# Pairs 14 and 15 computed first and plain in the up projection, the Strassen pairs 0 to 13 after them

## The chip, the cores and the metric

One core of a Trainium2 chip runs the kernel. The metric is the time of the device in microseconds; the median of several runs is compared. TensorE is called PE in the profile, VectorE DVE, ScalarE ACT, GpSimd POOL, and SyncE, which issues every DMA here, SP.

## What is computed

One decoder layer on 1024 tokens of 1024 features in float32. The part that matters is its second half, the MLP, and the norms about it:

```
h = rmsnorm(x, norm_ffn_g[l])
x = x + jnp.square(jax.nn.relu(h @ w_ffn_up[l])) @ w_ffn_down[l]
...
return rmsnorm(x, norm_final_g)
```

The hidden width is 4096, that is 32 tiles of 128, or 16 pairs of tiles.

## The kernel before

The first half (norm, input projection, attention, convolution, output projection) is not touched. Every product of float32 matrices is made of three matmuls of rounded parts (`mm3`, lines 58 to 61): high with high, high with low, low with high. The high part is rounded by ACT (line 55), the low part is the difference and is made by DVE or POOL (line 56, the split).

The up projection goes over 16 pairs of hidden tiles. A pair with its two halves of tokens is a 2 x 2 block product, and 14 pairs are computed by a Strassen scheme with seven products instead of eight (`up7`, line 986, products u1 to u7 of 12 matmuls of 128x512 each). The scheme needs sums of the activations as moving operands (t1s, t2s, t4s and new contents of h2h[1] and h2l[1]). They are built from a copy of the activations in DRAM (`hraw`), in `make_moving` (line 966) and `make_t3` (line 975): loads into the seven buffers `tmp`, subtractions on POOL, rounding on ACT, low parts on DVE. Until they are there, two pairs are computed plainly (`up_plain`, line 917, with `up_half`, eight products' worth of matmuls); before the change these are pairs 0 and 1. `NPL = 2` at line 1067 is their number.

What a pair yields goes to DRAM in `hid[1]` to `hid[7]`, in the form in which the down projection needs it. `sums_up` (line 895) makes it: four squared blocks a11, a21, a12, a22 in the tile `work_q`, and four sums s1 to s4 of them in `work_s` (lines 906, 907, 908, 914, on DVE), seven stores in all. For pairs 14 and 15 the sums are left out and four blocks are stored plainly (`plain`, line 899).

The down projection takes two pairs as a group: eight groups, of which the first seven use a Strassen scheme again, and the last, group 7 of pairs 14 and 15, is plain and is fused with the last norm (`final`). `SEQ0`, `SEQ`, `SEQN` give the order of the seven products of a group. For each product, `load_b` and `load_h` fetch a weight block b and a hidden block h, `prep` (line 1057) splits both into high and low, and `products` (line 1129) makes four token tiles in two PSUM tiles of two banks each, named dn + group + product + first token tile (dn060 and dn062 are product 6 of group 0). There are four such PSUM tiles at a time (`ps_two`, line 865). Products 1, 6 and 7 of group 0 are copied to `xe` by ACT (line 1138); all others are added by DVE to an accumulator (line 1140): products 2 and 3 to the tiles xr0 and xr1, products 4 and 5 to xr2 and xr3, one for each two token tiles. These four hold x, which `reload_x2` (line 1111) fetches from DRAM again, since their memory was lent out during the up projection: xr0's to `work_q`, xr1's to `work_s` (line 881), those of xr2 and xr3 to t4s. Line 1160 subtracts the accumulators from each other once, when product 5 of group 0 is due.

`begin_down` (line 1082) is called in the last pair after its third product, and loads and splits the first blocks of group 0.

Within each engine the order of instructions is settled when the program is built, by a scheduler that follows its own estimate of time; DMAs are issued by SP in such an order too, and an instruction that waits holds up those behind it on its engine.

Of the kernel before, what the change touches and what calls it, by code (L numbers as in the profile page):

```python
# [33 lines left out]
def body(tc, x, norm_mix_g, w_in, b_forget, conv_dw_w, conv_dw_b, conv_ln_g, conv_ln_b,  # L34
# [19 lines left out]
    def split(hi, lo, src, eng=V):  # L54
        A.activation(hi, src, AF.Copy)  # L55
        eng.tensor_tensor(lo, src, f32(hi), op=ALU.subtract)  # L56

    def mm3(ps, sh, sl, mh, ml, first, last):
        T.matmul(ps, sh, mh, start=first, stop=False)  # L59
        T.matmul(ps, sh, ml, start=False, stop=False)  # L60
        T.matmul(ps, sl, mh, start=False, stop=last)  # L61
# [4 lines left out]
    def ps_mm(name):  # L66
        return psum.tile([P, HN], F32, tag="mm", name=name, bufs=4)
# [669 lines left out]
    for t in range(NT):  # L737
        n = CV0 + CVS * t
# [23 lines left out]
    with tc.manual_schedule(engines={mybir.EngineType.PE}):  # L762
        for n in range(START, len(units) + 30):
# [4 lines left out]
            if 0 <= n < len(units):  # L768
                weighted_v(n, *prs.pop(n))
                h, hf, kt = units[n]  # L770
# [17 lines left out]
    def load_w2(src, name, shape, scale=None):  # L788
        hi = wgt.tile(shape, F32R, tag="hi", name=name + "h", bufs=3)
        lo = wgt.tile(shape, F32R, tag="lo", name=name + "l", bufs=3)  # L790
        half = shape[1] // 2
        for k in range(0, shape[1], half):
            raw = wgt.tile([P, half, shape[2]], F32, tag="raw", name=f"{name}r{k}", bufs=3)
            SP.dma_start(raw, src[:, k:k + half, :])
            if scale is None:
                split(hi[:, k:k + half, :], lo[:, k:k + half, :], raw)
            else:
                for j in range(half):
                    A.activation(hi[:, k + j, :], raw[:, j, :], AF.Copy, scale=chan(scale, k + j))
                    V.scalar_tensor_tensor(lo[:, k + j, :], raw[:, j, :], chan(scale, k + j), f32(hi[:, k + j, :]),  # L800
                                           op0=ALU.mult, op1=ALU.subtract)
        return hi, lo
# [44 lines left out]
    def norm_cols2(t):  # L847
        xn = xns.pop(t)
        pt = ps_big(f"n2_{t}_t")
        for k in range(KT):  # L850
            T.transpose(pt[:, k * P:(k + 1) * P], xn[:, k * P:(k + 1) * P], ident)
        hf, c = t // 4, (t % 4) * P
        split(h2h[hf][:, :, c:c + P], h2l[hf][:, :, c:c + P], pt.rearrange("p (k n) -> p k n", k=KT))
        A.activation(x2[t], pt, AF.Copy)
        SP.dma_start(hraw[:, :, t * P:(t + 1) * P].rearrange("k p n -> p k n"), x2[t].rearrange("p (k n) -> p k n", k=KT))
# [9 lines left out]
    def ps_two(name):  # L865
        return psum.tile([P, 2, HN], F32, tag="two", name=name, bufs=4)

    NPAIR = NFF // 2
# [6 lines left out]
    def load_up(j):  # L875
        return load_w2(w_up_k[:, :, j * P:(j + 2) * P], f"up{j}", [P, KT, 2 * P])
# [3 lines left out]
    def open_work():  # L880
        work["q"] = x2p.tile([P, 2, 2, HN], F32, tag="x0", name="work_q", bufs=1)
        work["s"] = x2p.tile([P, 4, HN], F32, tag="x1", name="work_s", bufs=1)

    def up_half(p, w, e, hf, ps):
        sl = slice(e * P, (e + 1) * P)
        for k in range(KT):
            mm3(ps, w[0][:, k, sl], w[1][:, k, sl], h2h[hf][:, k, :], h2l[hf][:, k, :], k == 0, k == KT - 1)
        q = work["q"][:, e, hf, :]
        A.activation(q, ps, AF.Relu)
        A.activation(q, q, AF.Square)  # L890
# [4 lines left out]
    def sums_up(p, last):  # L895
        q, sm = work["q"], work["s"]
        a11, a21, a12, a22 = q[:, 0, 0, :], q[:, 0, 1, :], q[:, 1, 0, :], q[:, 1, 1, :]
        s1, s2, s3, s4 = [sm[:, i, :] for i in range(4)]
        plain = p >= NPAIR - 2
        if not last:  # L900
            store(p, 1, a11)
            store(p, 4, a22)
            if plain:
                store(p, 0, a21)
                return
            V.tensor_tensor(s1, a21, a22, op=ALU.add)
            V.tensor_tensor(s2, s1, a11, op=ALU.subtract)
            V.tensor_tensor(s3, a11, a21, op=ALU.subtract)
            for i, a in ((5, s1), (6, s2), (7, s3)):
                store(p, i, a)  # L910
        else:
            store(p, 2, a12)
            if not plain:
                V.tensor_tensor(s4, a12, s2, op=ALU.subtract)
                store(p, 3, s4)

    def up_plain(p, w, hfs):
        for hf in hfs:
            for e in range(2):
                up_half(p, w, e, hf, ps_two(f"up{p}{e}{hf}")[:, 0, :])  # L920
            if (p, hf) == (NPL - 1, 1):
                for k in range(4):
                    make_t3(k)
        sums_up(p, False)
        sums_up(p, True)

    def load_up7(p):
        g = [wgt.tile([P, 2, 4, P], F32, tag="raw", name=f"ur{p}{i}", bufs=3) for i in range(3)]
        ah, al, bh, bl = [wgt.tile([P, 4, 4, P], F32R, tag=tg, name=f"u{tg}{p}{c}", bufs=3) for c in "ab" for tg in ("hi", "lo")]
        c0 = 2 * p * P  # L930
        for dst, k0, e in ((g[2][:, 0], 0, 1), (g[2][:, 1], 4, 1), (g[0][:, 0], 0, 0), (g[1][:, 1], 4, 0)):
            SP.dma_start(dst, w_up_k[:, k0:k0 + 4, c0 + e * P:c0 + (e + 1) * P])
        G.tensor_tensor(g[0][:, 1], g[2][:, 0], g[2][:, 1], op=ALU.add)  # L933
        G.tensor_tensor(g[1][:, 0], g[0][:, 1], g[0][:, 0], op=ALU.subtract)
        G.tensor_tensor(g[2][:, 0], g[0][:, 0], g[2][:, 0], op=ALU.subtract)
        split(ah[:, 0:2], al[:, 0:2], g[0])
        split(ah[:, 2:4], al[:, 2:4], g[1])
        G.tensor_tensor(g[1][:, 1], g[1][:, 1], g[1][:, 0], op=ALU.subtract)  # L938
        split(bh[:, 0], bl[:, 0], g[1][:, 1])
        split(bh[:, 1:3], bl[:, 1:3], g[2])  # L940
        w = {1: (ah, al, 0), 5: (ah, al, 1), 6: (ah, al, 2), 2: (ah, al, 3), 3: (bh, bl, 0), 7: (bh, bl, 1), 4: (bh, bl, 2)}
        return {i: (h[:, j], l[:, j]) for i, (h, l, j) in w.items()}
# [15 lines left out]
    def tmp(name):  # L958
        return tp.tile([P, HN], F32, tag="tmp", name=name, bufs=7)
# [15 lines left out]
    def make_t3(k):  # L975
        b12, b22 = load_hraw(f"c12_{k}", k, 1), load_hraw(f"c22_{k}", 4 + k, 1)
        G.tensor_tensor(b12, b22, b12, op=ALU.subtract)
        split(*mov[7][k], b12)

    def prod(p, w, i):  # L980
        ps = ps_two(f"u{i}_{p}")[:, 0, :]
        for k in range(4):
            mm3(ps, w[i][0][:, k, :], w[i][1][:, k, :], *mov[i][k], k == 0, k == 3)
        return ps

    def up7(p, w, mid=None):
        q = work["q"]
        s1, s5, u2 = tmp(f"us1_{p}"), tmp(f"us5_{p}"), tmp(f"uu2_{p}")

        def relu2(dst, ps, other):  # L990
            V.tensor_tensor(dst, ps, other, op=ALU.add)  # L991
            V.scalar_tensor_tensor(dst, dst, 0.0, dst, op0=ALU.max, op1=ALU.mult)  # L992

        A.activation(s1, prod(p, w, 1), AF.Copy)
        A.activation(s5, prod(p, w, 5), AF.Copy)
        V.tensor_tensor(u2, prod(p, w, 6), s1, op=ALU.add)
        if mid is not None:
            mid()
        G.tensor_tensor(s5, s5, u2, op=ALU.add)
        relu2(q[:, 0, 0, :], prod(p, w, 2), s1)  # L1000
        relu2(q[:, 0, 1, :], prod(p, w, 3), s5)
        p7 = prod(p, w, 7)
        V.tensor_tensor(u2, p7, u2, op=ALU.add)
        relu2(q[:, 1, 1, :], p7, s5)
        sums_up(p, False)
        relu2(q[:, 1, 0, :], prod(p, w, 4), u2)
        sums_up(p, True)
# [57 lines left out]
        return hi, lo  # L1065

    NPL = 2
    uws = {0: load_up(0)}
    open_work()
    for e in range(2):  # L1070
        up_half(0, uws[0], e, 0, ps_mm(f"up0{e}0"))
    norm_cols2(NT - 1)
    pn.release()
    psum.release()
# [15 lines left out]
        load_h(0, SEQ0[3])  # L1090
        ready[0] = prep(*steps[0])

    for p in range(NPAIR):
        if p + 1 < NPAIR:
            uws[p + 1] = load_up(2 * p + 2) if p + 1 < NPL else load_up7(p + 1)
        if p < NPL:
            for k in range(2 * p, 2 * p + 2):
                make_moving(k)
            up_plain(p, uws.pop(p), (1, 0) if p else (1,))
        else:  # L1100
            up7(p, uws.pop(p), begin_down if p == NPAIR - 1 else None)
    tp.release()
    hp.release()

# [137 lines left out]
```

## Time and profile before

| | us |
|---|---|
| median of 3 runs | 1165.04 |
| lowest and highest run | 1164.96 and 1166.43 |
| the profiled execution | 1163.59 |
| its span, from the first to the last instruction | 1161.9 |
| PE busy | 1123.3 |
| DVE busy | 913.7 |
| ACT busy | 471.6 |
| POOL busy | 466.1 |

The span is one execution on the chip taken by the profiler; the execution's own time is 1.7 us longer than the span. A busy time is the sum of an engine's instructions, over stages that are limited by different things, so the stretch at hand has to be looked at. In this execution the up projection begins at about 515 us of the span, its Strassen pairs at 568, and the down projection at 838.

### The profile page before, as it was taken

The numbers are of one execution on the slowest core, as the hardware profiler recorded it, in microseconds if no ns is written. First come the engines' busy times: TensorE is split into PE (matmuls) and PEld (weight loads), VectorE is DVE, ScalarE is ACT, GpSimd is POOL, SyncE is SP. The second block draws the span as 40 slices with busy tenths as digits, with TensorE's granted clock in tenths as the row PEclk, the third lists the DMA queues.
The fourth block names the chain that finished last, engine by engine and source line by source line (L and its number), as shares of the span: only waits on it lengthen the run. The fifth ranks groups of instructions, "written<-read, shape, count | busy, mean of one in ns | idle before, by whom it ended". The sixth has DMA issues, their size and how long they took to land. (4 is left out here: it accounts for less than half of the span.)

```text
span 1161.9 us, 15112 instructions
## 1 busy us (share of the span) xinstructions
PE 1123.3 (97%) x5455; PEld 915.3 (79%) x5455; DVE 913.7 (79%) x1147; ACT 471.6 (41%) x723; POOL 466.1 (40%) x358
## 2 busy tenths in 40 slices
PE   6999999999999999999899999999999999999997
PEld 6899888866677778887688888888877888888876
DVE  5399999666888765565887878787699988888994
ACT  6322353128788932364422222222253333333422
POOL 6122254116878820124743434343263434352021
PEclk9999999999999999999999999999999999999999
DMA  8021136683423333456644444444694454445003
GB/s 260 16 74 37 37 83 155 174 234 92 128 83 87 105 129 125 141 170 209 217 143 163 137 163 142 158 146 171 223 396 149 162 175 156 142 137 173 27 23 123
DMA packets 121779, 164.52 MB, mean 142 GB/s; under 512 B 9112, under 2 KB 66792, under 8 KB 121704
## 3 DMA queue, kind: packets, MB, share of 16 engines
q1 hardware_dynamic: 121704, 163.56, 43.5%
q8 instruction: 43, 0.70, 0.2%
q14 instruction: 32, 0.26, 0.1%
HBM read 114.67 MB, written 48.79 MB: 141 GB/s over the span
## 5 line engine op out<-in xcount | busy, mean ns | idle before, releaser
L292 DVE SCALAR_TENSOR_TENSOR conv<-u,par,conv 128x1024 f32<-128x1024 f32 x108 | 133.7, 1280 | 1.7 <-ACT conv L287 1.3
L1140 DVE TENSOR_TENSOR xr<-dn,xr 128x1024 f32<-128x1024 f32 x56 | 67.8, 1217 | 22.6 <-PE dn L61 22.6
L56 POOL TENSOR_TENSOR pl<-pt,ph 128x512 fp32r<-128x512 f32 (+3 forms) x71 | 74.6, 1066 | 25.3 <-ACT ph L55 22.2
L938 POOL TENSOR_TENSOR ur<-ur 128x512 f32<-128x512 f32 x14 | 23.1, 1647 | 95.4 <-DVE ulo10a L56 7.4
L613 ACT ACTIVATE pt<-sT,ctok 128x512 f32<-128x512 f32 (+1 forms) x96 | 54.5, 585 | 11.5 <-PE sT L611 5.8
L992 DVE SCALAR_TENSOR_TENSOR work_q<-work_q 128x512 f32<-128x512 f32 x56 | 53.1, 947 | 1.0
L453 DVE CUSTOM_DVE_ANT_0 mj<-s,ck 128x512 bf16<-128x512 f32 (+2 forms) x64 | 37.4, 585 | 18.6 <-PE s L447 11.6
L991 DVE TENSOR_TENSOR work_q<-u,us 128x512 f32<-128x512 f32 x42 | 28.6, 681 | 26.7 <-PE u L61 26.7
L55 ACT ACTIVATE ph<-pt 128x512 fp32r<-128x512 f32 (+1 forms) x96 | 48.7, 530 | 0.6
L1140 DVE TENSOR_TENSOR xe<-dn,xe 128x1024 f32<-128x1024 f32 x36 | 42.8, 1213 | 3.6 <-PE dn L61 3.6
L82 POOL TENSOR_SCALAR rs_tmp<-n_ss 128x1 f32<-128x1 f32 x16 | 5.6, 347 | 87.5 <-ACT n_xn L116 80.6
L59 PE MATMUL qk<-hTh,wh_qk 128*128 128x512 f32 x96 | 39.0, 406 | 0.0
L60 PE MATMUL qk<-hTl,wh_qk 128*128 128x512 f32 x96 | 37.9, 395 | 0.0
L61 PE MATMUL qk<-hTh,wl_qk 128*128 128x512 f32 x96 | 37.8, 394 | 0.0
L445 PE MATMUL s<-ks,q 128*128 128x512 f32 (+2 forms) x96 | 36.6, 388 | 0.9 <-DVE m L453 0.8
L633 PE MATMUL av<-pl,v 128*65 128x512 f32 (+1 forms) x96 | 32.5, 339 | 3.9 <-POOL pl L56 2.3
L61 PE MATMUL v<-wh_v,hTl 128*128 128x260 f32 x128 | 36.1, 282 | 0.0
L60 PE MATMUL v<-wl_v,hTh 128*128 128x260 f32 x128 | 36.1, 282 | 0.0
L59 PE MATMUL v<-wh_v,hTh 128*128 128x260 f32 x128 | 36.0, 281 | 0.0
L631 PE MATMUL av<-ph,v 128*65 128x512 f32 (+1 forms) x96 | 35.3, 368 | 0.1
L933 POOL TENSOR_TENSOR ur<-ur 128x512 f32<-128x512 f32 x14 | 24.0, 1717 | 24.8 <-DVE up2l L56 3.0
L608 PE MATMUL sT<-q,ks 128*128 128x512 f32 (+1 forms) x96 | 33.6, 350 | 0.1
(1315 smaller groups left out, 3908.1 us busy)
## 6 DMA issues: line engine op xcount, KB each, us to landing
h<-hid SPq DMA_DIRECT2D x53, 512.0 KB
b<-in_w_ffn_down SPq DMA_DIRECT2D x32, 512.0 KB
ur<-in_w_ffn_up SPq DMA_DIRECT2D x56, 256.0 KB
hid<-work_s SPq DMA_DIRECT2D x56, 256.0 KB
hid<-work_q SPq DMA_DIRECT2D x50, 256.0 KB
xp<-in_x SPq DMA_DIRECT2D x8, 512.0 KB
qstack<-qk SPq DMA_DIRECT2D x32, 128.0 KB
kstack<-qk SPq DMA_DIRECT2D x32, 128.0 KB
```

What stands on the lines that cost most here:

```text
L55: A.activation(hi, src, AF.Copy)
L56: eng.tensor_tensor(lo, src, f32(hi), op=ALU.subtract)
L59: T.matmul(ps, sh, mh, start=first, stop=False)
L60: T.matmul(ps, sh, ml, start=False, stop=False)
L61: T.matmul(ps, sl, mh, start=False, stop=last)
L292: V.scalar_tensor_tensor(dst, u[:, k:k + S], tap_w(c, k), cell[0], op0=ALU.mult, op1=ALU.add)
L445: T.matmul(ps[:, :w], d["q2"][:, i * P:(i + 1) * P], d["ks"][:, b0:b1], start=True, stop=b1 < n)
L453: V.tensor_tensor_reduce(junk[:, :w], ps[:, :w], d["ck"][:, b0:b1], op0=ALU.subtract, op1=ALU.max, scale=1.0, scalar=d.pop("m0") if b0 els ...
L613: A.activation(pt[:, :w], ps[:, :w], AF.Exp, bias=ctok[:, h * NT + kt:h * NT + kt + 1])
L631: T.matmul(av[:DH + 1, o0:], v1, ph[:, :w], start=kt == ORDER[hf][0], stop=False)
L992: V.scalar_tensor_tensor(dst, dst, 0.0, dst, op0=ALU.max, op1=ALU.mult)
L1140: V.tensor_tensor(a, ps, a, op=ALU.add)
```

## The change

The order of the pairs becomes 14, 15, 0, 1, ..., 13, and the two pairs computed plainly are 14 and 15. Their weights are both requested before the loop (the call for the second was in the loop), and `up_plain` is told by a flag, no longer by the pair's number, when to make the last moving operands. With it, the pairs that are plain in the up projection are those that have no sums, and the last two pairs of the up projection, now 12 and 13, have them.

```diff
@@ -914,11 +914,11 @@
                 V.tensor_tensor(s4, a12, s2, op=ALU.subtract)
                 store(p, 3, s4)
 
-    def up_plain(p, w, hfs):
+    def up_plain(p, w, hfs, last):
         for hf in hfs:
             for e in range(2):
                 up_half(p, w, e, hf, ps_two(f"up{p}{e}{hf}")[:, 0, :])
-            if (p, hf) == (NPL - 1, 1):
+            if last and hf == 1:
                 for k in range(4):
                     make_t3(k)
         sums_up(p, False)
@@ -1065,10 +1065,12 @@
         return hi, lo
 
     NPL = 2
-    uws = {0: load_up(0)}
+    order = list(range(NPAIR - NPL, NPAIR)) + list(range(NPAIR - NPL))
+    pa, pb = order[:NPL]
+    uws = {pa: load_up(2 * pa), pb: load_up(2 * pb)}
     open_work()
     for e in range(2):
-        up_half(0, uws[0], e, 0, ps_mm(f"up0{e}0"))
+        up_half(pa, uws[pa], e, 0, ps_mm(f"up{pa}{e}0"))
     norm_cols2(NT - 1)
     pn.release()
     psum.release()
@@ -1090,15 +1092,15 @@
         load_h(0, SEQ0[3])
         ready[0] = prep(*steps[0])
 
-    for p in range(NPAIR):
-        if p + 1 < NPAIR:
-            uws[p + 1] = load_up(2 * p + 2) if p + 1 < NPL else load_up7(p + 1)
-        if p < NPL:
-            for k in range(2 * p, 2 * p + 2):
+    for n, p in enumerate(order):
+        if NPL - 1 <= n < NPAIR - 1:
+            uws[order[n + 1]] = load_up7(order[n + 1])
+        if n < NPL:
+            for k in range(2 * n, 2 * n + 2):
                 make_moving(k)
-            up_plain(p, uws.pop(p), (1, 0) if p else (1,))
+            up_plain(p, uws.pop(p), (1, 0) if n else (1,), n == NPL - 1)
         else:
-            up7(p, uws.pop(p), begin_down if p == NPAIR - 1 else None)
+            up7(p, uws.pop(p), begin_down if n == NPAIR - 1 else None)
     tp.release()
     hp.release()
```

In the order of the built program, PE, ACT and POOL keep their instructions in place, with other names. Only on DVE and SP do instructions move, in two stretches of the program.

The first is DVE while the moving operands are built (b and c are loads of hraw; t1s, t2s, t4s and h2l1 the operands). The piece before the change:

```order
L56 TENSOR_TENSOR t2s_5599<-b11_2_5738,t2s_5599 128x512
L906 TENSOR_TENSOR work_s_5522<-work_q_5521 128x512
L907 TENSOR_TENSOR work_s_5522<-work_s_5522,work_q_5521 128x512
L56 TENSOR_TENSOR t1s_5598<-b00_3_5751,t1s_5598 128x512
L914 TENSOR_TENSOR work_s_5522<-work_q_5521,work_s_5522 128x512
L56 TENSOR_TENSOR t4s1_5601<-b10_2_5740,t4s1_5601 128x512
L56 TENSOR_TENSOR t2s_5599<-b11_3_5755,t2s_5599 128x512
L56 TENSOR_TENSOR h2l1_5108<-c12_0_5822,h2h1_5106 128x512
L906 TENSOR_TENSOR work_s_5522<-work_q_5521 128x512
L56 TENSOR_TENSOR t4s1_5601<-b10_3_5757,t4s1_5601 128x512
L56 TENSOR_TENSOR h2l1_5108<-c12_1_5829,h2h1_5106 128x512
L56 TENSOR_TENSOR h2l1_5108<-c12_2_5836,h2h1_5106 128x512
```

The same piece after it:

```order
L56 TENSOR_TENSOR t2s_5609<-b11_2_5731,t2s_5609 128x512
L56 TENSOR_TENSOR t1s_5608<-b00_3_5744,t1s_5608 128x512
L56 TENSOR_TENSOR t4s1_5611<-b10_2_5733,t4s1_5611 128x512
L56 TENSOR_TENSOR t2s_5609<-b11_3_5748,t2s_5609 128x512
L56 TENSOR_TENSOR h2l1_5108<-c12_0_5815,h2h1_5106 128x512
L56 TENSOR_TENSOR t4s1_5611<-b10_3_5750,t4s1_5611 128x512
L56 TENSOR_TENSOR h2l1_5108<-c12_1_5822,h2h1_5106 128x512
L56 TENSOR_TENSOR h2l1_5108<-c12_2_5829,h2h1_5106 128x512
```

The sums into work_s (lines 906, 907, 914, and 908 just ahead of the piece) are gone from between the splits.

The second is DVE at the start of the down projection, from the last split for product 3 on (d06lo, d07lo, d05lo are low parts for products 6, 7, 5; line 1140 has become 1142 and 1160 has become 1162). Before:

```order
L56 TENSOR_TENSOR d06lo_7974<-h6_0_7805,d06hi_7973 128x1024
L56 TENSOR_TENSOR d06lo_7974<-t2_0_7913,d06hi_7973 128x1024
L1140 TENSOR_TENSOR xr1_7897<-dn022_7993,xr1_7897 128x2x512
L56 TENSOR_TENSOR d07lo_8008<-h7_0_7900,d07hi_8007 128x1024
L56 TENSOR_TENSOR d07lo_8008<-b12_0_7803,d07hi_8007 128x1024
L1140 TENSOR_TENSOR xr1_7897<-dn032_8027,xr1_7897 128x2x512
```

and, after four rows that are left out here:

```order
L56 TENSOR_TENSOR d04lo_8076<-t2_0_7913,d04hi_8075 128x1024
L56 TENSOR_TENSOR d11lo_8118<-h1_1_7931,d11hi_8117 128x1024
L1140 TENSOR_TENSOR xr3_7905<-dn052_8137,xr3_7905 128x2x512
L56 TENSOR_TENSOR d16lo_8152<-h6_1_7933,d16hi_8151 128x1024
L1140 TENSOR_TENSOR xr0_7894<-dn020_7979,xr0_7894 128x2x512
L1140 TENSOR_TENSOR xr0_7894<-dn030_8013,xr0_7894 128x2x512
```

After:

```order
L907 TENSOR_TENSOR work_s_5532<-work_s_5532,work_q_5531 128x512
L914 TENSOR_TENSOR work_s_5532<-work_q_5531,work_s_5532 128x512
L56 TENSOR_TENSOR d06lo_7974<-h6_0_7798,d06hi_7973 128x1024
L56 TENSOR_TENSOR d06lo_7974<-t2_0_7913,d06hi_7973 128x1024
L56 TENSOR_TENSOR d07lo_8008<-h7_0_7900,d07hi_8007 128x1024
L56 TENSOR_TENSOR d07lo_8008<-b12_0_7796,d07hi_8007 128x1024
L56 TENSOR_TENSOR d05lo_8042<-h5_0_7908,d05hi_8041 128x1024
L56 TENSOR_TENSOR d05lo_8042<-t1_0_7912,d05hi_8041 128x1024
L1142 TENSOR_TENSOR xr0_7894<-dn020_7979,xr0_7894 128x2x512
L1142 TENSOR_TENSOR xr0_7894<-dn030_8013,xr0_7894 128x2x512
L1162 TENSOR_TENSOR xr0_7894<-xr0_7894,xr2_7902 128x2x512
L1142 TENSOR_TENSOR xr1_7897<-dn022_7993,xr1_7897 128x2x512
```

Two of the last pair's sums stand ahead of the splits (its other two a little earlier), the adds of dn022 and dn032 into xr1 have gone behind the splits, and behind the adds of dn020 and dn030 into xr0, which stood last.

The third is SP in that stretch: the stores of the last pairs (hid), the loads of group 0 (b and h with _0), and the reloads of xr. Before, the piece with the reload of xr1:

```order
L893 DMA hid2_5504<-work_q_5521 128x512
L893 DMA hid3_5505<-work_s_5522 128x512
L1115 DMA xr1_7897<-x2d_5115 128x1024 x2
L893 DMA hid1_5503<-work_q_5521 128x512
L893 DMA hid0_5510<-work_q_5521 128x512
L893 DMA hid4_5506<-work_q_5521 128x512
L893 DMA hid2_5504<-work_q_5521 128x512
L1027 DMA b11_0_7791<-in_w_ffn_down 128x2x512
L1033 DMA h1_0_7793<-hid1_5503 128x2x512
```

and, later, the piece with the reload of xr0:

```order
L1033 DMA h4_1_7939<-hid4_5506 128x2x512
L1033 DMA h3_1_7941<-hid3_5505 128x2x512
L1115 DMA xr0_7894<-x2d_5115 128x1024 x2
L1033 DMA h2_1_7943<-hid2_5504 128x2x512
L1027 DMA b11_2_8191<-in_w_ffn_down 128x2x512
L1027 DMA b12_2_8193<-in_w_ffn_down 128x2x512
L1033 DMA h1_2_8199<-hid1_5503 128x2x512
```

After, the piece with both:

```order
L1033 DMA h4_1_7939<-hid4_5506 128x2x512
L1033 DMA h3_1_7941<-hid3_5505 128x2x512
L1117 DMA xr0_7894<-x2d_5115 128x1024 x2
L1033 DMA h2_1_7943<-hid2_5504 128x2x512
L1027 DMA b11_2_8191<-in_w_ffn_down 128x2x512
L1027 DMA b12_2_8193<-in_w_ffn_down 128x2x512
L1117 DMA xr1_7897<-x2d_5115 128x1024 x2
L1033 DMA h1_2_8199<-hid1_5503 128x2x512
```

The reload of xr1 has moved from ahead of all loads of the down projection to a place behind b12 of group 2. Ahead of xr0, the last pair has seven stores where it had four.

## Rows read from the trace of the kernel before

**Rows 1.** the page, part 1: busy us (share of the span) xinstructions of each engine.

```profile
PE 1123.3 (97%) x5455; PEld 915.3 (79%) x5455; DVE 913.7 (79%) x1147; ACT 471.6 (41%) x723; POOL 466.1 (40%) x358
```

**Rows 2.** timeline of PE: start us, us, engine line op out<-in [idle before <-releaser].

```profile
573.25 0.80 PE L59 MATMUL u<-t2s,uhi2a 128*128 128x512 f32 x1 [4.62 <-ACT work_q L889]
...
576.30 0.39 PE L60 MATMUL u<-t2s,uhi2a 128*128 128x512 f32 x1
```

**Rows 3.** busy time by stretch: us of PE, PEld, DVE, ACT, POOL, then PEclk, DMA, GB/s.

```profile
574.00:576.00 2.00, 2.00 (x7) 1.52 (x6) 2.00 (x5) 2.00 (x3) 0.00 (x0) 0.50 0.53 199
```

**Rows 4.** timeline of PE, at the first plain pair.

```profile
529.14 0.50 PE L59 MATMUL up<-h2h,up0h 128*128 128x512 f32 x1 [1.39 <-ACT h2h L55]
...
530.96 0.40 PE L59 MATMUL up<-h2h,up0h 128*128 128x512 f32 x1
```

**Rows 5.** timeline of ACT, the read that frees u6's buffer.

```profile
572.62 0.58 ACT L889 ACTIVATE work_q<-up 128x512 f32<-128x512 f32 x1
```

**Rows 6.** timeline of POOL, make_t3 of the second and third k.

```profile
567.75 1.79 POOL L977 TENSOR_TENSOR c<-c,c 128x512 f32<-128x512 f32 x1 [1.68 <-DMA c<-hraw]
...
570.42 1.64 POOL L977 TENSOR_TENSOR c<-c,c 128x512 f32<-128x512 f32 x1 [0.87 <-DMA c<-hraw]
```

**Rows 7.** timeline of DVE, the start of its run and the plain pairs' sums.

```profile
539.84 1.22 DVE L56 TENSOR_TENSOR t1s<-b,t1s 128x512 fp32r<-128x512 f32 x1 [9.50 <-ACT t1s L55]
...
542.69 1.77 DVE L908 TENSOR_TENSOR work_s<-work_q 128x512 f32<-128x512 f32 x1
...
556.34 1.77 DVE L906 TENSOR_TENSOR work_s<-work_q 128x512 f32<-128x512 f32 x1
...
558.14 1.67 DVE L907 TENSOR_TENSOR work_s<-work_s,work_q 128x512 f32<-128x512 f32 x1
...
561.43 1.78 DVE L914 TENSOR_TENSOR work_s<-work_q,work_s 128x512 f32<-128x512 f32 x1
...
567.14 0.68 DVE L906 TENSOR_TENSOR work_s<-work_q 128x512 f32<-128x512 f32 x1
```

**Rows 8.** timeline of PE, products 6, 5 and 4 of group 0.

```profile
854.88 0.39 PE L59 MATMUL dn<-d06hi 128*128 128x512 f32 x1
...
866.87 0.50 PE L60 MATMUL dn<-d05lo,d05hi 128*128 128x512 f32 x1 [0.54 <-DVE d05lo L56]
...
873.70 0.50 PE L59 MATMUL dn<-d04hi 128*128 128x512 f32 x1 [1.32 <-DVE xr L1140]
```

**Rows 9.** busy time by stretch, from the down projection's first loads on.

```profile
826.00:830.00 4.00, 4.00 (x19) 3.27 (x18) 0.69 (x1) 1.06 (x1) 1.33 (x2) 1.00 0.59 201
...
830.00:834.00 4.00, 4.00 (x20) 3.30 (x19) 3.46 (x4) 2.10 (x2) 2.33 (x1) 1.00 1.04 353
...
830.00:842.00 12.00, 12.00 (x55) 9.93 (x54) 11.43 (x11) 5.82 (x6) 7.06 (x3) 1.00 1.03 371
...
842.00:854.00 12.00, 12.00 (x55) 9.76 (x54) 12.00 (x7) 5.34 (x6) 8.49 (x4) 1.00 1.04 405
...
854.00:866.00 12.00, 12.00 (x54) 9.66 (x52) 12.00 (x6) 6.87 (x7) 9.26 (x4) 1.00 1.05 390
```

**Rows 10.** timeline of DVE in the same stretch.

```profile
851.68 1.21 DVE L1140 TENSOR_TENSOR xr<-dn,xr 128x1024 f32<-128x1024 f32 x1
...
860.06 3.42 DVE L1160 TENSOR_TENSOR xr<-xr,xr 128x1024 f32<-128x1024 f32 x1
...
863.40 3.42 DVE L56 TENSOR_TENSOR d05lo<-t,d05hi 128x1024 fp32r<-128x1024 f32 x1
```

**Rows 11.** timeline of SP: loads of group 0, and the reload of xr0.

```profile
824.94 0.38 SPq L1027 DMA_DIRECT2D b<-in_w_ffn_down  x1
...
827.75 0.37 SPq L1033 DMA_DIRECT2D h<-hid  x1
...
856.90 1.95 SPq L1115 DMA_DIRECT2D xr<-x2d  x2
```

**Rows 12.** timeline of ACT, the first use of h1 of group 0.

```profile
831.54 1.06 ACT L55 ACTIVATE d01hi<-h 128x1024 fp32r<-128x1024 f32 x1 [1.91 <-DMA h<-hid]
```

## The prediction

> **What bounds the kernel now.** I read the page first. TensorE is busy for 97% of the span [rows 1], so a change pays or costs where TensorE waits. I then listed TensorE in order of time around the two ends of the up projection, and behind each wait the engine that ended it. Three waits matter.
>
> The first is at the start of the Strassen products. The third product, u6, waits 4.62 us for a PSUM buffer that ScalarE has yet to read (line 889), and then runs slowly: seven matmuls take from 573.25 to 576.30, 3.05 us, where seven at the usual spacing of 0.227 us take 1.59 [rows 2]. The granted clock of that stretch is 0.50, the level of 1.2 GHz instead of 2.4 [rows 3]. So this wait costs 4.62 + 1.46 = 6.08 us. A shorter wait of 1.39 us, at 529.14, was followed by matmuls of the usual 0.40 us [rows 4]. ScalarE reads that buffer only at 572.62 [rows 5], because ahead of it stand two copies for the moving operands (make_t3), and these wait for GpSimd. GpSimd stood idle 1.68 and 0.87 us for the loads of c12 and c22 [rows 6]. The loads are late since their buffers come free only as VectorE works through its queue, without a pause from 539.84 on. Five of its instructions up to 568 are sums of the two plain pairs (lines 906, 907, 908, 914), 0.7 to 1.8 us each, 7.7 us in all [rows 7].
>
> The second and third waits are 0.54 and 1.32 us in the first group of the down projection [rows 8]. There VectorE has no pause either, and the DMA engines run without a gap at 371 to 405 GB/s [rows 9].
>
> **The change, part by part.** The arithmetic stays the same: the same products, fourteen pairs with sums, two without. TensorE's, ScalarE's and GpSimd's order are unchanged but for names, so what the work of these engines costs is 0. The earlier call for the second plain weight moves no DMA past another, 0 as well. What moves are eight sums on VectorE and some transfers on SP.
>
> *The start.* The plain pairs lose their eight sums and three stores each. Price for TensorE: at least nothing (the loads stay late for another reason), at most the whole 6.08 us. With 7.7 us of VectorE's queue gone the c loads can be issued early enough; GpSimd's idle 1.68 + 0.87 = 2.55 us then go. The wait of 4.62 us therefore shrinks by something between 2.55 and 4.62; I take the middle, 3.6. About 1.0 us is left, less than the 1.39 us after which TensorE kept its speed [rows 4], so the 1.46 us of slow matmuls go too. Sum: **-5.1 us**. Everything behind it is earlier by as much.
>
> *Pair 12* does four sums where pair 14 did none. Twelve of the Strassen pairs before carry the same four sums, and the list of TensorE's waits has none between u6 of the first pair and the 0.54 us of the down projection: 0, hidden under the products.
>
> *The last Strassen pair, 13,* is the dear part. It has four sums, work_s stays in use until its last store has landed, and work_s lies in the memory into which xr1 is reloaded. In the order of the program this turns two things round. The reload of xr1, which stood ahead of the down projection's loads, now stands behind the load of b12_2. And VectorE no longer adds dn022 and dn032 into xr1 between the splits for products 6, 7 and 5; it now does all these splits, then dn020 and dn030 into xr0, and only then xr1.
>
> PSUM holds four half products. dn010, dn012, dn020 and dn022 fill it; ScalarE empties the first two, for dn030 and dn032; dn060 must wait until VectorE has added dn020 or dn022. Before, dn022 was added at 851.68 [rows 10], and dn060 began at 854.88 without a wait [rows 8]. Now dn020 is first, and it needs two things.
>
> (a) VectorE's turn. The split of t1 for product 5 ended at 863.40 + 3.42 = 866.8 [rows 10]. From this go the 5.1 us of the start and what now stands behind: two adds into xr1 (2 x 1.21, one of them shown) and the subtraction (3.42), 5.8 us [rows 10]. To it come four sums of 0.68 to 1.78 us [rows 7], 2.7 to 7.1. It ends between 858.6 and 863.0.
>
> (b) The reload of xr0. SP issued it at 856.90, behind a backlog [rows 11]. From the first load of the down projection (824.94) to xr0, 27 transfers of 512 KB and 4 of 256 KB were issued, 15.2 MB. The engines moved, by the stretches [rows 9] and some 0.2 MB in the microsecond before them, 0.2 + 0.80 + 4.45 + 4.86 + 4.68 = 15.0 MB up to 866.0, so xr0 was through at 866.5. Pair 13 puts seven stores into this line where pair 15 put four: 0.79 MB more, 2.0 us at 0.39 MB/us. So 868.5, less the 5.1 of the start: 863.4. How long after that VectorE sees it, no row shows directly. The nearest is h1: issued at 827.75 [rows 11], used at 831.54 [rows 12]. Of these 3.79 us the issue is 0.37 and its own 0.52 MB at 371 GB/s 1.41, which leaves 2.0; if b11, issued 2.8 us earlier, was still all in front of it, 0.6. I take 2.0: 865.4. Even the earliest value, 864.0, is later than (a), so the load decides.
>
> The Trainium skill (DMA: Bandwidth & Descriptors, section "Where 436 GB/s comes from") says that between HBM and SBUF the HBM side binds, at some 358 GB/s for a core. The rows show more, up to 405 [rows 9], so I sum by the rows; by the page's figure the 15.0 MB that follow the first megabyte would take 41.9 us instead of 38.5, and the load would come 3.4 us later.
>
> The add of dn020 takes 1.2 us, as the one at 851.68 did, so dn060 starts at 866.6 instead of 854.88: +11.7, on the absolute scale, the 5.1 us already inside. TensorE has then stood idle for some 17 us (it was ready at 849.8) and will run slowly for a while; the row with 4.62 us idle lost 1.46 by it, so +1.5 (bounds 0 and 3). The two waits of 0.54 and 1.32 us go, since the buffers are by then handed back in order: -1.9 (at the least 0).
>
> *xr1.* Its reload is issued when the split of t1 is done (b12_2 takes t1's buffer), by 863.0, and moves behind h2, b11_2 and b12_2: five transfers of 0.52 MB, 6.7 us behind xr0, so it is there at 872.1. dn022 is added by 873.3. TensorE wants that buffer for the fourth half product from dn060 on, three halves of 12 x 0.227 = 2.72 us and the slow start later: 876. Cost 0, with 3 us to spare. From the second group on the order is the old one: 0.
>
> **Sum:** +11.7 + 1.5 - 1.9 = **+11.3 us**. The profiled execution took 1163.59 us, so 1174.9 there. The median of the runs, 1165.04, is 1.45 us above it, and I add the same: 1176.3.
>
> **The rivals.**
> *The load lands early and VectorE decides.* If the DMA engines bring xr0 before its place in the line, dn060 starts 1.2 us after (a), 859.8 to 864.2: +4.9 to +9.3, less 0.4 for the other two terms: 1169.5 to 1173.9. For it: stores and loads may overtake each other. Against: 100% busy DMA, and loads of which all are needed. Chance 0.17.
> *The line moves slower.* The additional stores write HBM while the loads read it. At 353 GB/s, the lowest stretch with all DMA engines busy [rows 9], those 15.0 MB take 42.5 us, 4.0 more: 1180.3. The page's 358 GB/s, cited above, would give 1179.7. Chance 0.13.
> *The start gives nothing.* If u6's wait is set by the hraw loads and GpSimd alone, the 5.1 us do not come off, here or at xr0: 1181.4. Against it: VectorE's unbroken run [rows 7]. Chance 0.09.
> *Faster.* The add of dn020 does not hold TensorE at all. It decides at one point: it must be done by 849.8, when dn032 ends. Then only the start is left, 1165.04 - 5.1 = 1159.9. The printed order is against it: six splits and two sums stand ahead of that add since the last TensorE product of the pair, and its load is far down the line. Chance 0.04.
> *The two ends cancel* within 0.2%, the 2.3 us that a measurement of this kernel can tell from no change: 0.02.
>
> **How the numbers follow.** My case has 0.55, the other slower ones 0.39. The range goes from the low end of the VectorE case to just above the case without a gain at the start: 1169.5 to 1182. Faster 0.04, same 0.02, slower 0.94.
>
> **What would show it.** u6's wait under 1.5 us, and full-speed matmuls behind it; dn010 some 5 us earlier; then one wait of 14 to 18 us before dn060, ended by VectorE's add into xr (or by its DMA), with the add itself waiting for the reload; half the usual clock for a few matmuls after it; no further wait of over 1 us up to dn110. I am wrong in the mechanism if dn060 starts without a wait or if the wait sits at another product, and wrong in a size if VectorE is found busy, rather than waiting for DMA, right before the add.

## The result, and the profile after

The change makes the kernel slower: 1179.3 us median (1177.45 to 1180.92, 4 runs) against 1165.3 for the kernel before in the same comparison; ratio 1.0116, 95% interval 1.0102 to 1.0129. The profiled execution took 1177.45 us, 13.86 more than the one of before. The forecast was 1176.3, within 1169.5 to 1182.

The engines do the same work; VectorE's busy time is 6.1 us less and GpSimd's 2.7 us [rows 1]. From the page, part 1:

```profile
PE 1123.1 (96%) x5455; PEld 915.3 (78%) x5455; DVE 907.6 (77%) x1147; ACT 471.0 (40%) x723; POOL 463.4 (39%) x358
```

TensorE's busy time is the same, while the span grew from 1161.9 to 1175.7 us, so the loss is TensorE waiting. Its timeline, at u6 and u2 of the first Strassen pair, then from the first matmul of the down projection to the first of its group 1:

```profile
569.45 0.50 PE L59 MATMUL u<-t2s,uhi0a 128*128 128x512 f32 x1 [1.52 <-ACT work_q L889]
...
574.12 0.50 PE L59 MATMUL u<-h2h,uhi0a 128*128 128x512 f32 x1 [1.60 <-ACT work_q L889]
...
835.26 0.39 PE L59 MATMUL dn<-d01hi 128*128 128x512 f32 x1
...
847.44 0.50 PE L60 MATMUL dn<-d03lo,d03hi 128*128 128x512 f32 x1 [0.91 <-DVE d03lo L56]
...
869.93 0.76 PE L59 MATMUL dn<-d06hi 128*128 128x512 f32 x1 [16.98 <-DVE xr L1142]
...
872.94 0.40 PE L60 MATMUL dn<-d06lo,d06hi 128*128 128x512 f32 x1
...
893.16 0.39 PE L59 MATMUL dn<-d11hi 128*128 128x512 f32 x1
```

The wait of 4.62 us before u6 [rows 2] is now 1.52, and a second one, 1.60 before u2, has come up. Before dn060, where there was none [rows 8], stands the new wait of 16.98 us. Who ends it is seen on VectorE: the four sums of the last pair, the last split for product 5, and the two adds into xr0 and into xr1:

```profile
834.85 0.67 DVE L908 TENSOR_TENSOR work_s<-work_q 128x512 f32<-128x512 f32 x1
...
844.98 0.68 DVE L906 TENSOR_TENSOR work_s<-work_q 128x512 f32<-128x512 f32 x1
...
847.31 0.68 DVE L907 TENSOR_TENSOR work_s<-work_s,work_q 128x512 f32<-128x512 f32 x1
848.03 0.69 DVE L914 TENSOR_TENSOR work_s<-work_q,work_s 128x512 f32<-128x512 f32 x1
...
858.63 3.36 DVE L56 TENSOR_TENSOR d05lo<-t,d05hi 128x1024 fp32r<-128x1024 f32 x1
868.56 2.35 DVE L1142 TENSOR_TENSOR xr<-dn,xr 128x1024 f32<-128x1024 f32 x2 [6.57 <-DMA xr<-x2d]
...
876.08 2.35 DVE L1142 TENSOR_TENSOR xr<-dn,xr 128x1024 f32<-128x1024 f32 x2 [3.91 <-DMA xr<-x2d]
```

VectorE, which had no pause here before (12.00 us busy of 12 from 854 to 866 [rows 9]), stands idle for 6.57 us in front of the add that TensorE waits for: the reload of xr0 is late. (The second wait of 3.91 us, for xr1, holds nobody.) On SP, that reload still stands behind the loads of group 1, and xr1's stands behind it:

```profile
851.52 5.27 SPq L1033 DMA_DIRECT2D h<-hid  x5
857.07 0.99 SPq L1117 DMA_DIRECT2D xr<-x2d  x2
...
860.39 2.00 SPq L1027 DMA_DIRECT2D b<-in_w_ffn_down  x2
863.10 1.69 SPq L1117 DMA_DIRECT2D xr<-x2d  x2
```

The busy time by stretch, as in [rows 9] (PEclk, DMA share and GB/s are the last three columns):

```profile
830.00:842.00 12.00, 12.00 (x54) 9.94 (x54) 11.97 (x9) 5.90 (x7) 9.22 (x4) 1.00 1.05 400
...
842.00:854.00 12.00, 10.04 (x43) 7.64 (x42) 11.96 (x11) 4.84 (x6) 4.90 (x2) 1.00 0.92 326
854.00:866.00 12.00, 0.00 (x0) 0.00 (x0) 7.99 (x3) 0.99 (x2) 9.33 (x4) 0.57 1.04 394
...
844.00:846.00 2.00, 2.00 (x11) 1.65 (x10) 2.00 (x3) 0.00 (x0) 0.00 (x0) 1.00 0.66 247
846.00:848.00 2.00, 1.09 (x5) 0.59 (x4) 1.99 (x3) 1.66 (x2) 0.00 (x0) 1.00 0.76 219
```

From 830 to 842 and from 854 to 866, with every DMA engine busy, the line runs at about 400 GB/s, no slower than before. But it ran partly dry from 844 to 848, which it did not before (405 GB/s from 842 to 854).

To place each run's gain and loss I cut the timeline of TensorE at three points: the first matmul behind the transposes of the up projection (the row with 1.39 us idle, [rows 4]), the first matmul of dn010, and the first of dn110. From dn110 to the end of the span it is 282.5 to 282.6 us in all eight profiled executions: nothing that the change does reaches further.

| order of the pairs, and edit | start of the stage | from there to dn010 | dn010 to dn110 | wait before dn060 |
|---|---|---|---|---|
| before (0, 1, ..., 15) | 529.14 | 309.32 | 40.85 | none |
| the change (14, 15, 0, ..., 13) | 528.43 | 306.83 | 57.90 | 16.98 |
| 15, 0, ..., 14 | 531.04 | 306.56 | 42.71 | none |
| 0, 1, 14, 15, 2, ..., 13 | 529.66 | 310.64 | 58.56 | 17.46 |
| 0, 15, 1, ..., 14 | 529.76 | 310.58 | 42.52 | none |
| the change, sums in tmp | 528.98 | 305.99 | 45.78 | none |
| the change, xr0 ahead of h | 529.18 | 306.32 | 52.42 | 10.32 |
| the change, last sums left out | 527.89 | 306.21 | 43.16 | none |

For the change: -0.71 us that were there before the stage began, -2.49 in the up projection, +17.05 at the start of the down projection; 13.85 together. Each row is one execution: the stage begins between 527.89 and 531.04, and among the four rows with both plain pairs free of sums its length differs by up to 0.84 us, so differences of that size are not read as effects.

### The profile page after: what moved, and what is told of

It reads as the page before. It is cut to its first block, busy times and chain, and to the rows that moved or that the text cites. A ratio compares the mean times of both kernels' runs of the same rounds, so it can differ in the third digit from the quotient of the medians.

```text
span 1175.7 us, 15110 instructions
## 1 busy us (share of the span) xinstructions
PE 1123.1 (96%) x5455; PEld 915.3 (78%) x5455; DVE 907.6 (77%) x1147; ACT 471.0 (40%) x723; POOL 463.4 (39%) x358
## 5 line engine op out<-in xcount | busy, mean ns | idle before, releaser
L453 DVE CUSTOM_DVE_ANT_0 mj<-s,ck 128x512 bf16<-128x512 f32 (+2 forms) x64 | 37.4, 584 | 19.2 <-PE s L447 12.2
```

The costliest lines, as they stand in the source:

```text
L453: V.tensor_tensor_reduce(junk[:, :w], ps[:, :w], d["ck"][:, b0:b1], op0=ALU.subtract, op1=ALU.max, scale=1.0, scalar=d.pop("m0") if b0 els ...
```

## The experiments

Theory: the change is two independent parts. Plain pairs without sums give some 3 us at the start. A last Strassen pair with sums costs some 17 us, because its sums hold work_s, because of that xr1's reload moves back, and VectorE then adds into xr0 first, whose reload is far down the DMA line. The rivals were the VectorE time of the sums, the additional stores, and an effect of the pairs brought forward.

### Each half alone

The start part without the late part; only the first of the two plain pairs is free of sums here:

```
-    order = list(range(NPAIR - NPL, NPAIR)) + list(range(NPAIR - NPL))
+    order = [NPAIR - 1] + list(range(NPAIR - 1))
```

> The order is 15, 0, 1, ..., 14: plain pairs 15 and 0 first, and pair 14, which has no sums, is the last Strassen pair; pair 13 with its sums is the last but one. Theory (the whole late cost hangs on sums in the last pair): the wait before dn060 is back below 2 us, the reload of xr1 stands ahead of the one of xr0 again, and of the gain at the start (3.2 us by dn010 in the changed kernel) half to all is left, since pair 0 still has its four sums in the plain stage: 1162 to 1164 us. Rival (any Strassen pair with sums near the transition, or the plain pairs' early stores, cost what the changed kernel lost): dn060 waits 10 us or more, 1172 to 1179 us.

Measured: 1162.71 us, ratio 0.9974 (0.9963 to 0.9985) against before. TensorE's waits of over 0.5 us from 565 us to dn110:

```profile
576.47 0.50 PE L59 MATMUL u<-h2h,uhi1a 128*128 128x512 f32 x1 [1.52 <-ACT work_q L889]
...
850.55 0.50 PE L60 MATMUL dn<-d03lo,d03hi 128*128 128x512 f32 x1 [1.24 <-DVE d03lo L56]
...
867.91 0.50 PE L60 MATMUL dn<-d05lo,d05hi 128*128 128x512 f32 x1 [0.52 <-DVE d05lo L56]
...
874.74 0.50 PE L59 MATMUL dn<-d04hi 128*128 128x512 f32 x1 [1.32 <-DVE xr L1142]
```

No wait before u6, none before dn060, and the last two are those of [rows 8]. This order is faster than both kernels, by the median of 12 runs; the profiled one, 1164.56 us, was among the slower of them. Of the gain to dn010 (2.76 us by the table) 1.86 is lost again up to dn110, where the wait of 1.24 us before dn030 is new.

The late part without the start part:

```
-    order = list(range(NPAIR - NPL, NPAIR)) + list(range(NPAIR - NPL))
+    order = [0, 1, NPAIR - 2, NPAIR - 1] + list(range(2, NPAIR - 2))
```

> The order is 0, 1, 14, 15, 2, ..., 13: the plain pairs are those of the kernel before, with their sums, and the last pair is 13 with its sums, as in the changed kernel. Theory (the two parts of the change are independent, and the late one costs some 17 us): the wait of 4.6 us in the plain stage is back, dn060 waits 16 to 18 us, and the time is 1179.3 + 3.2 = 1182.5 us (1181 to 1184). Rival (the late cost comes from what was brought forward at the start): dn060 waits below 3 us, 1165 to 1167 us.

Measured: 1183.12 us, ratio 1.0156 (1.0143 to 1.0169). Both waits are there:

```profile
574.86 0.80 PE L59 MATMUL u<-t2s,uhi14a 128*128 128x512 f32 x1 [5.71 <-ACT work_q L889]
...
875.51 0.76 PE L59 MATMUL dn<-d06hi 128*128 128x512 f32 x1 [17.46 <-DVE xr L1142]
```

Alone the parts give -0.26% and +1.56%, 1.30% together; the change gives 1.16% (1.02 to 1.29). With some 0.1% of uncertainty on each part they add up, and the late wait does not need what was brought forward at the start.

### What the last pair's sums do

The same sums and stores in other memory, so that work_s is free after pair 12:

```
-        s1, s2, s3, s4 = [sm[:, i, :] for i in range(4)]
+        if p == order[-1]:
+            if not last:
+                last_sums.extend(tmp(f"sum{i}") for i in range(4))
+            s1, s2, s3, s4 = last_sums
+        else:
+            s1, s2, s3, s4 = [sm[:, i, :] for i in range(4)]
```

> The changed kernel, but the four sums of the last pair lie in four tiles of the tmp pool in place of one tile of work_s; VectorE's sums, the stores and their bytes stay. Theory (what counts is the memory: the reload of xr1 takes the place of work_s and so waits for the last pair's sums and their stores): xr1 is reloaded before them and added first, the wait of 17 us before dn060 falls below 5 us, and the time is 1163 to 1168 us. Rival (VectorE's work for the four sums, or the four stores more in the DMA line): dn060 still waits 12 us or more, 1174 to 1179 us.

Measured: 1164.86 us, ratio 0.9994 (0.9984 to 1.0004). The wait before dn060 is gone, with all sums and stores in place:

```profile
856.26 0.39 PE L59 MATMUL dn<-d06hi 128*128 128x512 f32 x1
```

SP issues xr1's reload ahead of the first load of the down projection:

```profile
821.37 0.80 SPq L1123 DMA_DIRECT2D xr<-x2d  x2
822.21 0.43 SPq L1033 DMA_DIRECT2D b<-in_w_ffn_down  x1
```

and VectorE adds into xr1 between the splits:

```profile
852.08 1.21 DVE L1148 TENSOR_TENSOR xr<-dn,xr 128x1024 f32<-128x1024 f32 x1
```

What is left is a wait of 3.03 us before dn030, where VectorE's sums stand among the splits:

```profile
849.34 0.80 PE L60 MATMUL dn<-d03lo,d03hi 128*128 128x512 f32 x1 [3.03 <-DVE d03lo L56]
```

So of the 17.05 us that the change loses from dn010 to dn110, 4.93 are left; the memory that the sums lie in costs the other 12. The complement takes the sums away and keeps the seven stores:

```
+        if p == order[-1]:
+            if not last:
+                for i, a in ((1, a11), (7, a11), (4, a22), (5, a22), (6, a21)):
+                    store(p, i, a)
+            else:
+                store(p, 2, a12)
+                store(p, 3, a12)
+            return
```

> The changed kernel without the four sums of the last pair 13: blocks of work_q are stored in their place, so the seven stores and their bytes stay, and the output is not the reference's. Theory (the late cost is the reload of xr1 tied to work_s; the stores cost nothing of note): dn060 waits below 3 us, and the time is that of the kernel before less the whole gain at the start, 1160.5 to 1163.5 us, 1 to 4 us below the run with the sums in tmp tiles, which pays for their time on VectorE. Rival (three stores more in the DMA line hold the loads of the down projection): a wait of 5 us or more on a load in 840 to 880 us, 1167 us or more.

Measured: 1162.31 us, ratio 0.9979 (0.9968 to 0.9989), as expected; the largest wait of TensorE in the down projection's first group is 1.32 us, and there is none before dn060:

```profile
851.54 0.39 PE L59 MATMUL dn<-d06hi 128*128 128x512 f32 x1
```

The stores as such cost nothing that can be seen. The sums cost 0.15%, 1.7 us, when they do not hold work_s; the intervals of the two runs overlap a little, so this size is only just clear of nothing.

### Load or VectorE's turn

My main case and my first rival differed in what ends the wait before dn060. Here the reload of xr0 is put ahead of group 1's hidden blocks by an order on SyncE alone:

```
+        ld = SP.dma_start(d[i], src.rearrange("q p n -> p q n"))
+        if g == 1:
+            for r in reloads[:2]:
...
```

(the added dependency makes each such load follow the two reloads of xr0).

> The changed kernel, with one order more on SyncE: the loads of hidden blocks for group 1 are issued behind the reload of xr0, which before them were ahead of it (2.5 MB of them). Theory (of the 17 us before dn060, those beyond VectorE's own turn are the reload's place in the DMA line): xr0 is visible by VectorE's end of the last split of d05, dn060 starts at 863 to 865 us in place of 869.9, and the time falls by 3 to 7 us, to 1172 to 1176 us. Rival (VectorE's order alone holds dn060): dn060 stays within 1 us of 869.9 and the time at 1178 to 1180 us.

Measured: 1171.56 us, ratio 1.0054 (1.0041 to 1.0067), just below the expected range. SP now issues xr0 5.35 us earlier, and VectorE adds without waiting for it, right behind the last split of product 5; TensorE's row follows:

```profile
851.72 1.03 SPq L1121 DMA_DIRECT2D xr<-x2d  x2
```

```profile
859.09 3.36 DVE L56 TENSOR_TENSOR d05lo<-t,d05hi 128x1024 fp32r<-128x1024 f32 x1
862.37 2.34 DVE L1146 TENSOR_TENSOR xr<-dn,xr 128x1024 f32<-128x1024 f32 x2
```

```profile
863.73 0.76 PE L59 MATMUL dn<-d06hi 128*128 128x512 f32 x1 [10.32 <-DVE xr L1146]
```

Of the 17 us some 6.7 were the load; the other 10.3 are VectorE's turn, because its order puts all splits for products 6, 7 and 5 ahead of the add. This edit moved a little more than meant: SP's other loads shifted too, and the line did not run dry (388 GB/s from 842 to 854), so the 6.2 us by which dn060 is earlier are the place in the line and the dry stretch together.

### Which plain pair's sums cost at the start

```
-    order = list(range(NPAIR - NPL, NPAIR)) + list(range(NPAIR - NPL))
+    order = [0, NPAIR - 1] + list(range(1, NPAIR - 1))
```

> The order is 0, 15, 1, ..., 14: as in the run whose order is 15, 0, 1, ..., 14, the last pair is 14 without sums, but now pair 0 with its four sums is the first of the two plain ones, and 15 the second. Theory (at the start it is the sums of the first plain pair that count: they stand on VectorE among the splits of t1s, t2s and t4s that hold up GpSimd and then ScalarE's evacuation of the last plain half): the wait of 4 to 6 us before u6 is back, and the time is that of the kernel before, 1164 to 1167 us. Rival (only the number of sums in the stage counts, so either plain pair without sums gives the gain): the wait before u6 is below 2 us and the time 1161.5 to 1163.5 us.

Measured: 1168.13 us, ratio 1.0024 (1.0014 to 1.0034), 1 us above the expected range. The wait before u6 is back, and with it GpSimd's wait for a c load:

```profile
574.85 0.50 PE L59 MATMUL u<-t2s,uhi1a 128*128 128x512 f32 x1 [4.07 <-ACT work_q L889]
```

```profile
569.55 1.28 POOL L977 TENSOR_TENSOR c<-c,c 128x512 f32<-128x512 f32 x1 [3.43 <-DMA c<-hraw]
```

So the first plain pair's sums, on VectorE from 543 to 565 us in this run, are the ones that count; the second pair's may stay. That fits 15, 0, ..., 14, which has the whole gain in the stage with one pair without sums. A plain pair without sums also has three stores fewer on SP, and no run takes away the one without the other. The trace speaks for VectorE: SP issued the last store of a sum ahead of the three late c loads at 565.00, the loads at 566.70, and in between it waited for a buffer, until VectorE's split of t4s, which stands right behind the last sum of line 914, ended at 566.67. Why this run is 0.24% above before is not settled: its timeline is longer than before's by 1.26 us in the up projection and by 1.67 at the start of the down projection, where a wait of 1.25 us before dn030 is new, as in 15, 0, ..., 14, which also ends with pair 14.

## Why the prediction was right, step by step

**The start, -5.1 us:** right in the mechanism, too large. Measured -2.49 in the stage. dn010 came 3.2 us earlier, but 0.71 of that was there before the stage began. I took GpSimd's two waits for loads away and half of the rest of u6's wait; 1.52 us of it stayed. The two waits did go: GpSimd did the second and third c subtraction back to back, until 568.24. What is left before u6 is this work itself; ScalarE rounds its result and then reads u6's buffer, until 569.39. Before the last subtraction GpSimd waited, no longer for a load but for VectorE's split:

```profile
564.81 3.43 POOL L977 TENSOR_TENSOR c<-c,c 128x512 f32<-128x512 f32 x2
569.74 1.29 POOL L977 TENSOR_TENSOR c<-c,c 128x512 f32<-128x512 f32 x1 [1.50 <-DVE h2l L56]
```

```profile
568.81 0.58 ACT L889 ACTIVATE work_q<-up 128x512 f32<-128x512 f32 x1
```

The half clock behind u6 went, as forecast (the last three columns are PEclk, DMA share and GB/s):

```profile
569.00:575.00 6.00, 3.96 (x16) 2.92 (x17) 3.65 (x4) 4.93 (x8) 1.29 (x1) 1.00 0.12 45
```

That was partly luck: my ground was that the pause of 1.39 us in [rows 4] had cost no clock, and half of the eight profiled executions contradict it (last section). What I missed is the next wait in line. ScalarE's read for u2's buffer stands behind the rounding of the last c and two roundings of weights:

```profile
571.60 1.99 ACT L55 ACTIVATE uhi1a<-ur 128x1024 fp32r<-128x1024 f32 x2
573.50 0.58 ACT L889 ACTIVATE work_q<-up 128x512 f32<-128x512 f32 x1
```

It stood there before the change too, and ended at 576.76, but TensorE, held at u6 for 6 us, came to u2 only at 577.47. With u6 early, 1.60 us of it show. Waits before: 4.62 + 1.46 of slow matmuls; after: 1.52 + 1.60.

**Pair 12, 0:** right; there is no wait of TensorE between u2 of the first pair and the down projection.

**VectorE's turn, 858.6 to 863.0:** it ended at 858.63 + 3.36 = 862.0. The last pair's four sums took 2.72 us together, the low end of my 2.7 to 7.1. That it still ended late in the range has two parts: dn010 moved 1.9 us less than I took off here, and the six splits for products 6, 7 and 5, which I took as before, took 13.8 us in place of 12.2 (their durations added).

**xr0 visible at 865.4:** it was 868.56, and this is the step that carries the error of 3.3 us in dn060's place (869.93 against 866.6). The reload was issued at 857.07, hardly other than before [rows 11]. Three things and some smaller ones lie behind the 3.2 us. I had taken the full 5.1 us of the start off the line's end, but SP's first load of the down projection moved by 3.2, from 824.94 to 821.74: 1.9 us. The 0.2 MB that I counted for the microsecond before 826 are in no row, 0.5 us; in the kernel before:

```profile
824.00:826.00 2.00, 2.00 (x10) 1.58 (x10) 0.00 (x0) 0.60 (x1) 0.00 (x0) 1.00 0.00 1
```

And I treated the line as always full; from 844 to 848 it moved 233 GB/s instead of 400, 0.67 MB or 1.7 us. Ahead of this, SP had waited 3.0 us for VectorE's split of d03lo, until 845.05, before it could issue the next loads. The line's speed elsewhere was near what I took, not the same: 400 GB/s against 371 from 830 to 842, which gives 0.9 us back, and 364 against 395 from 848 to 856 with all DMA engines busy, which costs 0.6. By an estimate from the bytes moved in stretches of 2 us since the first load, the 16.0 MB were through at some 867.3; VectorE then saw xr0 about 1.3 us later, where I took 2.0. These sizes add up to the error, but they are worked out from the rows and not tried. What makes the line run dry is open: in 15, 0, ..., 14, where nothing waits before dn060, it moved only 339 GB/s from 842 to 854.

My sentence on the Trainium skill (DMA: Bandwidth & Descriptors, section "Where 436 GB/s comes from") gave 358 GB/s as what binds a core. The trace after is again above that where the line is full, 400 and 394 GB/s, and at 360 from 844 to 868, the dry stretch included. An estimate from that figure of the Trainium skill, 1179.7 for the median, came nearer to the measured 1179.3 than mine. It would have been right by luck, since most of what slowed this line was the dry stretch.

**Half clock, +1.5:** the matmuls from 869.93 to 872.94 took 3.01 us in place of 1.59, +1.42.

**The old waits, -1.9:** they went. The 0.91 us before dn030 are new, but lie ahead of the long wait and are swallowed by it. From dn060 to dn110 the timeline is 1.20 us shorter than before; my terms +1.5 and -1.9 gave 0.4. **xr1, 0:** right; it was visible at 876.08, not 872.1, and still nobody waited for it.

**The sum:** dn060 came 15.05 us later than before where I forecast 11.7, the stretch behind it was 0.8 us shorter than forecast, and so the profiled execution lost 13.86 against 11.3. Of the error of 2.6 us, 1.9 are the start. Counted from dn010 the forecast is 11.3 + 5.1 = 16.4 us and the measured loss 17.05; that this is so close is partly luck, 1.4 us too little up to dn060 and 0.8 too much behind it. The median lies 1.85 us above the profiled execution, where I added 1.45.

**The rivals.** VectorE did not decide in the change as made, but was only 6.57 us away from it; the run with xr0 ahead shows that. A line slowed by the additional stores: no; without the last sums but with the seven stores it moved 401 GB/s from 842 to 854. No gain at the start: no; the run with the old plain pairs shows a stage of 310.64 us against 306.83. Faster: no.

## What to carry to other kernels

When work moves to another place in a loop, ask what memory it holds there and what is loaded into that memory next: here four sums of 0.7 us brought a wait of 17 us, most of it because a reload into their tile moved back and turned VectorE's order round. Where the same operations are wanted without that cost, either choose which iteration comes last (15, 0, ..., 14, 0.26% faster than before, 0.15 to 0.37) or give the last iteration's results other memory. And when a wait is shortened, look at the next reader of the same engine: the second wait was hidden behind the first.

## What was not expected of the hardware

Behind the transposes TensorE is idle for 1.39 us, runs one matmul, and is idle for 0.76 us [rows 4]. I took it from before that such a pause leaves the clock alone. Of the eight profiled executions four show a half clock right behind it and four do not, with the same idle times. The change, and the run with xr0 ahead, whose instructions up to there are the same, over the same three microseconds:

```profile
530.00:533.00 3.00, 3.00 (x15) 2.44 (x14) 0.00 (x0) 0.69 (x1) 0.00 (x0) 1.00 0.61 186
```

```profile
530.00:533.00 3.00, 2.56 (x7) 2.05 (x8) 0.39 (x1) 1.02 (x1) 0.00 (x0) 0.63 0.55 188
```

7 matmuls instead of 15, at a granted clock of 0.63; by the 33rd matmul of the stage the second is 1.6 us behind the first (10.04 against 8.42 us from the stage's start). What decides between the two is open; the instructions up to there do not. Nor does it show in these two stage times: the run with the half clock came to dn010 in 306.32 us, the other in 306.83, since TensorE then waited less at u6 and u2. Also, the granted clock is already down while TensorE stands idle before dn060: 0.57 from 854 to 866, with no matmul in it.
